# Attention keys' low parts doubled over both row halves in a two-layer transformer trunk

## The chip, the cores and the metric

The kernel runs on one core of one Trainium2 chip. The metric is the device time of one execution, in microseconds. PE is the engine of matrix products (PEld its weight loads), DVE and ACT do elementwise work, POOL a little of it, and SP issues most DMAs.

## The reference

Two layers (`DEPTH = 2`) on 512 tokens of width 1024. In each layer five attentions run on the same input, and a gated sum of them is projected, added to the input and normalised. Then a mixture of 16 experts (two for each token) follows, and a second norm.

```python
def hybrid_mixer(h, ...):
    h = x @ w_in                       # queries, keys, values of all branches
    o_sb   = stick_breaking_attention(q, k, v)          # 4 heads of 64
    o_moba = moba_attention(q, k, v, slopes)            # 4 heads of 64, causal here
    o_mla  = mla_attention(c_q, c_kv, k_rope, ...)      # 4 heads of 96
    o_nsa  = nsa_attention(q, kv, gates, ...)           # 4 heads of 64, two sets of shared keys
    o_mem  = memory_cross_attention(q_mem, mem, w)      # 4 heads of 64, 256 keys
    for i, o in enumerate((o_sb, o_moba, o_mla, o_nsa, o_mem)):
        merged += sigmoid(x @ w_gate[i] + b_gate[i]) * (o @ w_br[i])
    return merged @ w_out
```

A score is `q . k * scale`, with a slope times the distance in some branches; the weights of a query are the softmax of its scores (in stick breaking, a running product).

## The kernel before

Products are made from split numbers: every operand is kept as a high part (rounded to the type that PE takes at full rate) and a low part (what is left), and a product is the sum of high x high, high x low and low x high. `hi` (line 93) makes a high part, a copy on ACT; `lo` (line 108) makes a low part, a subtraction on DVE.

**Projections.** `fm_tile` (line 154) makes one [128 columns, 512 tokens] tile of `x @ w`: 24 matmuls at line 161, each 512 columns wide. Weights are loaded by SP, split on ACT and DVE, and used once. The gates (`gates`, line 770) are of this kind.

**Queries and keys.** A head has 64 numbers, half the height of PE. `q_stack` (line 204) puts a head's high query parts into its 64 rows and the low parts into the other 64. `k_pair` (line 212) gets two heads' keys from one psum tile and makes three tiles of the tag `qk`: for each head a tile with its high parts in both halves, and one tile `kl` in which each head's low parts lie in its own half. So one product over 128 rows gives q_hi k_hi + q_lo k_hi, and a second one over 64 rows gives q_hi k_lo. `std_passes` (line 318) lists the two passes. The compressed sparse attention makes its keys in `nsa_qkv` (lines 684 to 693) and already doubles the low parts there, but uses them through the same two passes.

**Scores.** `score_block` (line 232) takes 128 queries against L keys: the passes go into one psum bank of the tag `s` (two banks), through `mm` at line 116. DVE makes the minimum (line 246 with distances, 249 without), ACT the exponential (251), DVE the reciprocal and the scaled rows `ne` (252 to 256). `to_pt` (line 259) transposes them on PE (line 124) into a bank `pt`, and ACT and DVE split them into `pth` and `ptl`. At a head's end `causal_pv` (line 299) multiplies them with the values. L is 128, 256, 384 and 512 for a head's four blocks in the causal branches and 256 for each block of the memory's. The stick-breaking branch (line 403) has its own softmax substitute but the same two passes; the 96-wide latent attention (line 592) has three passes of 96 rows and doesn't use `k_pair`.

**Order.** `mixer` (line 904) weaves three generators by strings of letters in `orders` (line 1610): the attention of one branch (a), the gates of the branch before (g) and the projections of the next branch (q). Within this a scheduler orders the instructions and puts in the waits; every engine then works in the order of its own queue. Tiles of one tag share a number of slots given in `BUFS` (line 1592); a new tile waits until a slot is free. `qk` has 14 slots of 2 KB a partition, in the pool that is open during a layer's attentions. Around the experts other pools take its place.

Of the kernel before, what the change touches and what calls it, by code (L numbers as in the profile page):

```python
# [10 lines left out]
F32R = mybir.dt.float32r  # L11
# [7 lines left out]
P = 128  # L19
D = 1024  # L20
S = 512
# [4 lines left out]
ALPHA = (2.0 * DEPTH) ** 0.25  # L26
# [4 lines left out]
CAP = 112  # L31
# [39 lines left out]
class Trunk:  # L71
# [13 lines left out]
    # ---------------------------------------------------------------- tiles  # L85
# [6 lines left out]
    # ---------------------------------------------------------------- split  # L92
# [33 lines left out]
    # -------------------------------------------------------------- weights  # L126
    def load_w(self, src, shape, tag="rw", pool=None):
        """One raw piece of up to 4 KB a partition."""
        t = self.sb(pool or self.wp, [P, 1024 if tag == "rw" else 256], tag)
        n = 1  # L130
        for x in shape:
            n *= x
        v = t[:, :n]
        if len(shape) == 2:
            v = v.rearrange("p (a b) -> p a b", a=shape[0])
        if src is not None:
            self.loaded = self.nc.sync.dma_start(v, src)
        return v

    def split_w(self, raw, tag="wh", eng="dve", pool=None):  # L140
        """raw [P, a, b] -> its high and low parts, in one slot."""
# [11 lines left out]
    # feature-major tile of x @ w[:, cols]: w_hl is ([P, 8, M], [P, 8, M])  # L153
# [11 lines left out]
    def fm_chunk(self, w, c0, use, n=2, cut=1):  # L165
        """128 n columns of x @ w, feature-major: use(j, psum) for each tile."""
# [5 lines left out]
    def tm_chunk(self, w, c0, use, x=None, nt=NT, outer="k"):  # L172
        """256 columns of x @ w, token-major: use(t, psum [P, 256]). Two token tiles to a bank."""
        xh, xl = (self.xh, self.xl) if x is None else x
        o = [self.ps("f") for _ in range(nt // 2)]
        hl = {}

        def part(g, kk, t):
# [6 lines left out]
            for m, (a, b) in enumerate(((xh, h), (xh, l), (xl, h))):  # L185
                # one start a bank: it clears the whole bank's written bits
# [14 lines left out]
    # ------------------------------------------------------------ QKV parts  # L201
    H2 = (slice(0, 64), slice(64, 128))

    def q_stack(self, ps, rows, scale):
        """64 psum rows, scaled: their high parts stay in place, their low parts take the other half."""
# [6 lines left out]
    def k_pair(self, ps, n=S):  # L212
        """Two heads' keys: high parts doubled over both halves, a tile a head; low parts in place."""
        kh = [self.sb(self.ap, [P, S], "qk", F32R) for _ in range(2)]
        kl = self.sb(self.ap, [P, S], "qk", F32R)
        for r, k in zip(self.H2, kh):
            other = self.H2[r.start == 0]
            self.hi(k[r, :n], ps[r, :n])
            self.hi(k[other, :n], ps[r, :n])
            self.lo(kl[r, :n], ps[r, :n], k[r, :n])  # L220
        return [(kh[0], kl, self.H2[0]), (kh[1], kl, self.H2[1])]

    def v_split(self, ps, nh=4):
        """psum [P tok, nh*64] -> [P, nh, (hi 64 | lo 64)]."""
# [6 lines left out]
    # ------------------------------------------------------------ attention  # L231
    def score_block(self, i, L, passes, strip, slope=1.0, gate=None, causal=False):
        """Normalised probabilities [P q, L] in SBUF (fp32)."""
# [25 lines left out]
    def to_pt(self, e, nb, dst):  # L259
        """nb blocks of e [P q, nb*128], transposed and split: dst(hl) gives [P, nb, 128] views."""  # L260
# [8 lines left out]
    def pv_out(self, pv, o32, at):  # L269
        """[V_hi | V_lo] halves added into rows `at` of o32."""  # L270
# [19 lines left out]
    def causal_dst(self, pt, i, rev=False):  # L290
        # key tile j of query block i lies at columns (i + 3 j) * 128
# [7 lines left out]
    def causal_pv(self, pv, pt, vt, start, stop):  # L299
        """vt(j): [P, 128] stationary for key tile j."""  # L300
# [17 lines left out]
    def std_passes(self, q, k, qr=None):  # L318
        """Stacked queries on doubled keys, then the high queries (rows qr) on low keys (rows r)."""
        kh, kl, r = k  # L320
        return [(lambda sl: q[:, sl], lambda sl: kh[:, sl]), (lambda sl: q[r, sl], lambda sl: kl[r, sl])]

    # ------------------------------------------------------------- branches
# [26 lines left out]
    class _K:  # L350
        """[:, k, columns] of a list of tiles."""
# [51 lines left out]
    def sb_att(self, l, out):  # L403
        nc = self.nc
        for pr in range(2):
            o32 = self.o_tile()
            out.append(o32)
            for hh in range(2):
# [3 lines left out]
                for i in range(NT):  # L412
# [9 lines left out]
                    # u[j]: what all keys from j on leave; a key takes the difference  # L422
# [38 lines left out]
    # MLA  # L461
    def mla_qkv(self, l):
# [5 lines left out]
        # c_q (two tiles) and c_kv, feature-major, with their squares  # L468
        for j, c0 in ((2, 1792), (0, 1536), (1, 1664)):
# [6 lines left out]
            # sums of squares, token-major  # L476
# [11 lines left out]
        # k_rope | its halves swapped | the gates of the sparse attention  # L488
# [13 lines left out]
        # k rope: x cos + swapped x (-+ sin)  # L502
# [29 lines left out]
        # w_ukv -> [nope 4x64 | v 4x64]  # L532
# [32 lines left out]
        # w_uq per head [nope 64 | rope 32 | swapped 32]  # L565
# [42 lines left out]
    # NSA  # L608
    def nsa_qkv(self, l):
        nc, A = self.nc, self.A  # L610
        w = A["w_in"][l]
        # positional rows: [16, 128] = (pair, (parity, d)), doubled over partitions
# [16 lines left out]
        for m in range(2):  # L629
            x = self.sb(self.ap, [P, 16, 32], "ne")  # L630
            r = self.H2[m]
            for b in range(2):
                # windows n = 0..30 of 32 tokens, stride 16; token 2 a + b of each
# [8 lines left out]
        for m, nm in enumerate(("w_phi_k1", "w_phi_v1")):  # L642
# [6 lines left out]
            # gelu (tanh form): x/2 (1 + tanh(c (x + 0.044715 x^3)))  # L649
# [18 lines left out]
        # k_c duplicated over both halves: [kc_hi | kc_lo]  # L668
# [7 lines left out]
        # v_c of head h in rows 32 h  # L676
# [35 lines left out]
    def nsa_att(self, l, out):  # L712
        nc = self.nc
        # compressed scores, all heads and blocks: [P q, i, h, 32]
# [30 lines left out]
        for pr in range(2):  # L745
            o32 = self.o_tile()
            out.append(o32)
            for hh in range(2):
# [3 lines left out]
                for m in range(2):  # L752
                    pt = self.pt_tiles()
                    for i in range(NT):
                        e = self.score_block(i, P * (i + 1), self.std_passes(q, self.nk[m] + (self.H2[hh],)),
# [13 lines left out]
    # ------------------------------------------------------- gates and out  # L769
    def gates(self, l, b, o, first):  # L770
        """Adds sigmoid(x Wg + bg) * (o Wb) to merged (without the 0.5), 128 columns a step."""
# [24 lines left out]
    # ---------------------------------------------------------------- setup  # L796
# [21 lines left out]
    def setup_rest(self):  # L818
        """The constants that nothing needs at once."""
# [11 lines left out]
    def layer_cols(self, l):  # L831
        """Per-partition columns: 40 halved gate biases, g_cq (2), g_ckv, ln1 g and b (8 each)."""
# [15 lines left out]
    def x_tile(self, src, t, tag="f"):  # L848
        """Token tile t [P, 1024] into the transposed split x."""
# [10 lines left out]
    def weave(parts, order):  # L860
        """Runs the steps of generators in an order of their names, then the rest of each."""
# [6 lines left out]
    def start(self, l):  # L868
        """The layer's transposed input, the memory's keys and values, and what needs a token tile at a time."""
# [52 lines left out]
    def fill_rows(self, n, after):  # L922
        """Something finite in an expert's rows: its unused slots are read too."""
# [4 lines left out]
    # ------------------------------------------- output projection and norms  # L928
    def norm(self, st, eps=LN_EPS):
        """From the statistics of rows: minus their mean, the inverse of their deviation, minus the product."""  # L930
# [22 lines left out]
    def w_out(self, l, h_dram):  # L953
        """Output projection, residual, the first norm and the router: h1 token-major, its rows sent to experts.

        Two token tiles at a time share each split row block of the weights; the last blocks finish one tile, then the other."""
# [77 lines left out]
    def rows_done(self, t, o, hr, gb, pool):  # L1034
        """From the products of a tile: its rows' norm, logits and places. Yields how much later to go on."""
# [43 lines left out]
    # ------------------------------------------------------------------ moe  # L1079
    def router_w(self, l, pool):  # L1080
        """Router weights with the norm's gain folded in, their column sums, and the bias that its shift and theirs give."""
# [20 lines left out]
    def logits_in(self, x, half, pool):  # L1102
        """Half of the rows' columns, transposed."""
# [8 lines left out]
    def logits(self, o, xT, half):  # L1112
        """Adds the part of half of the rows' columns to the psum of the router's products."""
# [16 lines left out]
    def first_max(self, v, mx):  # L1130
        """Places of the largest (mx) of v [P, 4]: their priorities, and in column 4 the first one's."""
# [551 lines left out]
```

## Time and profile before

| | before |
|---|---|
| median of 3 runs, us | 1750.81 (1747.84 to 1752.13) |
| profiled execution, span, us | 1752.8 (no other time is given for it) |
| PE busy, us | 1644.5, 94% |
| PE weight loads busy, us | 1280.7, 73% |
| DVE busy, us | 1245.2, 71% |
| ACT busy, us | 896.2, 51% |
| matmuls | 7936 |

Busy time of PE is not the same as work: the profile's matmul durations overlap, and a matmul that waits for its own weight load counts as busy. How long PE takes for something is read from the starts of the instructions that follow each other. The attentions of the first layer lie between about 25 and 525 us, those of the second between 875 and 1400 us; the gates of the last branch, the output projection and the experts follow each.

### The profile page before, as it was taken

To read this page: it belongs to the slowest core of one execution; us is meant where nothing else is said; L and a number is where in the kernel's file an instruction comes from. 1 tells how busy PE (TensorE), PEld (TensorE's weight loads), DVE (VectorE), ACT (ScalarE), POOL (GpSimd) and SP (SyncE) were. 2 spreads that over 40 slices of the span, in tenths; PEclk is the share of its full clock that TensorE was granted. 3 is DMA by queue.
4 is the path that set the end of the run, shared out by engine and by line. 5 is a ranking of instruction groups with operands and counts; after the bars stand their busy time and mean duration, and the time that the engine had idled before them with its cause. 6 is when DMAs were issued, how large, how long until landed. Compare 5 with 4: busy or idle time off the path is not lost. (4 is left out here: it accounts for less than half of the span.)

```text
span 1752.8 us, 22824 instructions
## 1 busy us (share of the span) xinstructions
PE 1644.5 (94%) x7936; PEld 1280.7 (73%) x7936; DVE 1245.2 (71%) x2488; ACT 896.2 (51%) x1689; POOL 356.1 (20%) x261
## 2 busy tenths in 40 slices
PE   8999999999999987999699999999999998789994
PEld 7777877787778766666587787778877786676672
DVE  6666647765784689988687746587666757898876
ACT  5544446344463434888456334454444524358872
POOL 0000011111212254333410000110101113533345
PEclk9999999999999998999799999999999999899997
DMA  8232222353329547997642232223322286499943
GB/s 249 60 91 72 65 71 61 112 132 106 105 62 312 196 159 253 387 379 245 196 132 60 70 84 66 75 60 95 88 78 61 68 293 191 147 315 382 375 161 129
DMA packets 254561, 273.60 MB, mean 156 GB/s; under 512 B 38666, under 2 KB 191360, under 8 KB 254432
## 3 DMA queue, kind: packets, MB, share of 16 engines
q1 hardware_dynamic: 241032, 223.98, 40.2%
q0 software_dynamic: 13312, 47.98, 7.9%
q8 instruction: 67, 1.10, 0.3%
q14 instruction: 62, 0.51, 0.1%
q10 hardware_dynamic: 88, 0.03, 0.0%
HBM read 239.18 MB, written 32.77 MB: 155 GB/s over the span
## 5 line engine op out<-in xcount | busy, mean ns | idle before, releaser
L161 PE MATMUL f<-xh,wh 128*128 128x512 f32 (+2 forms) x1920 | 634.9, 400 | 1.6 <-ACT xh L97 0.9
L161 PEld LDWEIGHTS f<-xh,wh 128*128 128x128 f32 (+1 forms) x1920 | 354.4, 188 | 85.0 <-issue 5.2
L161 PE MATMUL f<-xl,wh 128*128 128x512 f32 (+2 forms) x960 | 383.6, 400 | 0.0
L791 POOL TENSOR_TENSOR mg<-mg,gt 128x512 f32<-128x512 f32 x64 | 96.3, 1505 | 1005.8 <-DVE gt L790 965.4
L112 DVE TENSOR_TENSOR wh<-rw,wh 128x1024 fp32r<-128x1024 f32 (+3 forms) x172 | 228.1, 1332 | 50.1 <-ACT wh L97 48.7
L161 PEld LDWEIGHTS f<-xl,wh 128*128 128x128 f32 (+1 forms) x960 | 180.6, 188 | 41.4 <-issue 3.5
L97 ACT CAST wh<-rw 128x1024 fp32r<-128x1024 f32 (+3 forms) x178 | 178.7, 1012 | 46.7 <-PE f L187 13.9
L781 ACT ACTIVATE gt<-f,bgh 128x512 f32<-128x512 f32 x80 | 55.1, 688 | 209.1 <-PE f L161 199.7
L116 PE MATMUL f<-wh,xh 128*112 128x512 f32 (+1 forms) x564 | 156.0, 404 | 5.0 <-DVE xh L112 2.7
L97 ACT CAST pth<-pt 128x128 fp32r<-128x128 f32 (+1 forms) x192 | 77.2, 418 | 110.4 <-PE pt L124 104.0
L116 PE MATMUL s<-qk,qk 128*128 128x256 f32 (+11 forms) x416 | 130.0, 367 | 0.7 <-DVE st L246 0.7
L116 PE MATMUL f<-oh,bh 128*128 128x512 f32 x480 | 130.3, 398 | 0.1
L116 PEld LDWEIGHTS f<-wh,xh 128*112 128x112 f32 (+1 forms) x564 | 98.7, 180 | 36.1 <-DVE wh L112 3.7
L116 PE MATMUL f<-eh,xh 128*112 128x512 f32 (+1 forms) x396 | 110.1, 404 | 10.6 <-DVE eh L112 10.6
L112 DVE TENSOR_TENSOR ptl<-pt,pth 128x128 fp32r<-128x128 f32 (+1 forms) x192 | 89.2, 475 | 42.2 <-ACT pth L97 39.8
L790 DVE SCALAR_TENSOR_TENSOR gt<-gt,f 128x512 f32<-128x512 f32 x64 | 43.8, 684 | 103.6 <-PE f L116 103.0
L116 PEld LDWEIGHTS s<-qk,qk 64*128 64x128 f32 (+2 forms) x416 | 75.7, 189 | 47.6 <-issue 28.5
L97 ACT CAST wh<-rp 128x1024 fp32r<-128x1024 f32 x84 | 87.4, 1053 | 38.3 <-PE pt L116 24.0
L112 DVE TENSOR_TENSOR wh<-rp,wh 128x1024 fp32r<-128x1024 f32 x70 | 94.9, 1365 | 13.2 <-ACT wh L97 12.6
L116 PEld LDWEIGHTS f<-oh,bh 128*128 128x128 f32 x480 | 88.0, 188 | 20.4 <-issue 1.2
L116 PEld LDWEIGHTS f<-eh,xh 128*112 128x112 f32 (+1 forms) x396 | 68.8, 179 | 31.4 <-DVE eh L112 12.3
L124 PE MATMUL pt<-ident,ne 128*128 128x128 f32 x472 | 82.9, 277 | 4.1 <-DVE ne L426 1.6
(366 smaller groups left out, 2832.4 us busy)
## 6 DMA issues: line engine op xcount, KB each, us to landing
rp<-in_w_up_dram SPq DMA_DIRECT2D x96, 512.0 KB, 14.2
rw<-in_w_gate_dram SPq DMA_DIRECT2D x80, 512.0 KB, 3.9
rp<-in_w_down_dram SPq DMA_DIRECT2D x48, 512.0 KB, 13.7
rw<-in_w_in_dram SPq DMA_DIRECT2D x38, 512.0 KB, 3.9
rw<-in_w_out_dram SPq DMA_DIRECT2D x32, 512.0 KB, 4.7
yd<-xl POOLq DMA_DIRECT2D x28, 448.0 KB, 7.0
xl<-xd POOLq DMA_DIRECT2D x24, 448.0 KB, 7.6
rb<-in_w_br_dram SPq DMA_DIRECT2D x80, 128.0 KB, 3.4
```

Source lines behind the costliest of these rows:

```text
L97: return nc.scalar.copy(out, in_)
L112: return e.tensor_tensor(out, in_, hi.bitcast(F32), ALU.subtract)
L116: self.nc.tensor.matmul(out, lhsT, rhs, start=start, stop=stop)
L124: self.nc.tensor.transpose(out, in_, self.ident[:k, :k])
L161: self.nc.tensor.matmul(o[:M, n], a[:, k, :M], b[:, k, n], start=c + k + m == 0, stop=k == KT - 1 and m == 2, skip_group_check=cut > 1)
L781: nc.scalar.activation(t, gp, AF.Tanh, bias=self.bgh[:, b * 8 + f : b * 8 + f + 1], scale=0.5)
L790: nc.vector.scalar_tensor_tensor(t, t, 1.0, bp, ALU.add, ALU.mult)
L791: i = nc.gpsimd.tensor_tensor(m, m, t, ALU.add)
```

## The change

`k_pair` gives each head its own low tile with the low parts in both halves. For the memory's 256 keys, high and low parts share one tile of 512 columns. `std_passes` multiplies the whole query tile with both, so that the second pass gives q_hi k_lo + q_lo k_lo over 128 rows. The compressed attention hands over its key tiles as they are. `qk` has 18 slots. The rest of the diff takes out comments.

```diff
     def k_pair(self, ps, n=S):
-        kh = [self.sb(self.ap, [P, S], "qk", F32R) for _ in range(2)]
-        kl = self.sb(self.ap, [P, S], "qk", F32R)
-        for r, k in zip(self.H2, kh):
+        out = []
+        for r in self.H2:
             other = self.H2[r.start == 0]
-            self.hi(k[r, :n], ps[r, :n])
-            self.hi(k[other, :n], ps[r, :n])
-            self.lo(kl[r, :n], ps[r, :n], k[r, :n])
-        return [(kh[0], kl, self.H2[0]), (kh[1], kl, self.H2[1])]
+            t = [self.sb(self.ap, [P, S], "qk", F32R) for _ in range(S // n - 1 or 2)]
+            kh, kl = t if len(t) == 2 else (t[0][:, :n], t[0][:, n:])
+            for o in (r, other):
+                self.hi(kh[o, :n], ps[r, :n])
+            for o in (r, other):
+                self.lo(kl[o, :n], ps[r, :n], kh[r, :n])
+            out.append((kh, kl))
+        return out
...
-    def std_passes(self, q, k, qr=None):
-        kh, kl, r = k
-        return [(lambda sl: q[:, sl], lambda sl: kh[:, sl]), (lambda sl: q[r, sl], lambda sl: kl[r, sl])]
+    def std_passes(self, q, k):
+        return [(lambda sl: q[:, sl], lambda sl, x=x: x[:, sl]) for x in k]
...
-                        e = self.score_block(i, P * (i + 1), self.std_passes(q, self.nk[m] + (self.H2[hh],)),
+                        e = self.score_block(i, P * (i + 1), self.std_passes(q, self.nk[m]),
...
-    BUFS = dict(rb=2, bh=2, gt=2, oo=4, oh=2, qk=14, v=6, ne=3, st=6, ot=2, mt=3, cp=2, uw=3,
+    BUFS = dict(rb=2, bh=2, gt=2, oo=4, oh=2, qk=18, v=6, ne=3, st=6, ot=2, mt=3, cp=2, uw=3,
```

## Rows read from the trace of the kernel before

**Rows 1.** The page's first line.
```profile
span 1752.8 us, 22824 instructions
```

**Rows 2.** Busy time by stretch: length, busy us (x count) by engine, clock, DMA.
```profile
25.00:525.00 500.00, 496.81 (x2428) 389.67 (x2426) 337.63 (x790) 244.87 (x553) 46.48 (x39) 0.99 0.32 89
...
875.00:1400.00 525.00, 519.78 (x2571) 409.14 (x2571) 358.33 (x827) 256.75 (x567) 44.19 (x31) 0.99 0.28 78
```

**Rows 3.** Waits of PE, 25 to 525 us, the longest: total us, times, longest.
```profile
PE pt L124 <- DVE ne L426: 0.8, 2, 0.5
```

**Rows 4.** Score passes' weight loads by shape: busy, mean ns, idle before, its end.
```profile
L116 PEld LDWEIGHTS s<-qk,qk 128*128 128x128 f32 x160 | 30.1, 188 | 10.9 <-DVE st L246 2.4 <-issue 1.2 <-ACT ne L251 0.5
L116 PEld LDWEIGHTS s<-qk,qk 64*128 64x128 f32 x160 | 29.2, 183 | 33.5 <-issue 27.3
...
L116 PEld LDWEIGHTS s<-qk,qk 96*128 96x128 f32 x96 | 16.3, 199 | 3.3 <-ACT ne L251 1.5
```

**Rows 5.** Timeline, weight loads around a 384-wide block: start us, length us, instruction.
```profile
268.10 0.19 PEld L116 LDWEIGHTS s<-qk,qk 128*128 128x128 f32 x1
268.54 0.18 PEld L116 LDWEIGHTS s<-qk,qk 64*128 64x128 f32 x1 [0.25 <-issue]
268.91 0.19 PEld L116 LDWEIGHTS f<-cp,uw 128*128 128x128 f32 x1 [0.19 <-issue]
269.02 0.19 PEld L161 LDWEIGHTS f<-xh,wh 128*128 128x128 f32 x1
```

**Rows 6.** Timeline, matmuls around blocks of 384, 256 (two) and 128.
```profile
268.27 0.71 PE L116 MATMUL s<-qk,qk 128*128 128x384 f32 x2
268.92 0.50 PE L116 MATMUL f<-cp,uw 128*128 128x512 f32 x1
269.25 0.39 PE L161 MATMUL f<-xh,wh 128*128 128x512 f32 x1
269.48 0.39 PE L161 MATMUL f<-xl,wh 128*128 128x512 f32 x1
...
924.68 1.21 PE L116 MATMUL s<-qk,qk 128*128 128x256 f32 x4
925.83 0.50 PE L161 MATMUL f<-xh,wh 128*128 128x512 f32 x1
926.17 0.39 PE L161 MATMUL f<-xl,wh 128*128 128x512 f32 x1
...
188.96 0.48 PE L116 MATMUL s<-qk,qk 128*128 128x128 f32 x2
189.37 0.50 PE L161 MATMUL f<-xh,wh 128*128 128x512 f32 x1
189.70 0.39 PE L161 MATMUL f<-xl,wh 128*128 128x512 f32 x1
```

**Rows 7.** Timeline, matmuls of full height, 384 and 256 columns wide.
```profile
371.94 0.35 PE L116 MATMUL pv<-ptl,v 128*128 128x384 f32 x1
372.12 0.28 PE L116 MATMUL pv<-pth,v 128*128 128x256 f32 x1
372.24 0.28 PE L116 MATMUL pv<-ptl,v 128*128 128x256 f32 x1
```

**Rows 8.** Waits of the weight loader, 25 to 525 us: total us, times, longest.
```profile
PEld pv L116 <- ACT pth L97: 2.5, 11, 0.4
PEld pt L124 <- DVE ne L254: 1.5, 4, 0.9
...
PEld pv L116 <- DVE ptl L112: 1.2, 5, 0.4
```

**Rows 9.** Low parts on DVE by shape: count, busy us, mean ns, idle before.
```profile
L112 DVE TENSOR_TENSOR qk<-f,qk 64x512 fp32r<-64x512 f32 x32 | 21.9, 685 | 13.5 <-ACT qk L97 13.0
...
L112 DVE TENSOR_TENSOR qk<-f,qk 64x256 fp32r<-64x256 f32 x8 | 3.4, 421 | 1.1 <-ACT qk L97 1.0
```

**Rows 10.** Busy time where layer two starts, columns as in rows 2.
```profile
850.00:875.00 25.00, 17.52 (x71) 13.76 (x71) 19.15 (x40) 12.95 (x29) 8.75 (x6) 0.69 0.46 141
```

## The prediction

> **What bounds the kernel now.** I read the page first: one core, a span of 1752.8 us [rows 1]. The busy times by stretch come second [rows 2], because the change touches only the attention of the two layers, and that runs from about 25 to 525 us and from 875 to 1400 us. The reader is to see that PE is busy there for 496.8 of 500 us and 519.8 of 525 us, while DVE works for two thirds of that time and ACT for half. Third, the waits of PE in the first of these stretches: the longest group is 0.8 us in 500 [rows 3]. So in attention the end is set by how long PE takes for its own queue, and the question is whether all of that time is work.
>
> It is not. In the weight loads by shape [rows 4] the three heights of the score passes stand apart. The 160 loads that are 64 rows high have 33.5 us of idle loader time before them, and 27.3 us of it ended for no reason that the profile shows ("issue"). The 160 loads of full height, from the same line and the same tiles, have 1.2 us of that kind, and the 96 loads that are 96 rows high show none. The timeline of one 384-wide block says how it comes about [rows 5]. The full-height load at 268.10 is done when its matmul starts at 268.27 [rows 6]. The 64-row load for the second pass does not run ahead like that: it begins at 268.54, together with its own matmul. The full-height load behind it begins only at 268.91, again with its matmul. The next one, at 269.02, is early again. So going to the half height and coming back each leave a weight load uncovered, and PE waits for it while it counts as busy.
>
> **The change, part by part.** The first pass of each block stays as it is. The second pass takes the whole stacked query tile against low keys that lie in both halves, so it loads the full height, and no pass of the kernel's scores is 64 rows high any more. The number of matmuls and loads stays the same. What a pair of height changes costs is read from starts, because the durations overlap [rows 6]. Undisturbed, 512 columns follow each other every 0.23 us (269.25 to 269.48), 384 columns every 0.18 us and 256 columns every 0.12 us [rows 7]; for 128 columns I take the 0.12 us of 256, which is a ceiling.
> 384 wide: from 268.27, the start of the full pass, to 269.25, when the second matmul after the block starts, 0.98 us pass; undisturbed it would be 0.18 + 0.18 + 0.23 = 0.59, so 0.39 us are lost.
> 256 wide: two blocks and one matmul take 924.68 to 926.17 = 1.49 us, where 4 x 0.12 + 0.23 = 0.71 would do: 0.78, or 0.39 us a block.
> 128 wide: 188.96 to 189.70 = 0.74 us against 0.12 + 0.12 + 0.23 = 0.47: 0.27 us.
> 512 wide: I take the 0.39 us of 384, since 256 and 384 agree.
> The code has 16 such blocks in each of the memory, the stick-breaking and the block-sparse attention and 32 in the compressed one, 80 a layer, 160 in all, as the loads are counted [rows 4]. The memory's are all 256 wide; in the others the four widths come equally often. That makes 64 blocks of 256 and 32 of each other width: 128 x 0.39 + 32 x 0.27 = 58.6 us of PE time that goes. This is the main term.
>
> What is late next is the softmax chain: score, minimum, exponential, reciprocal, scaling, then the transposes and the probability products on PE. PE works off other blocks and projections meanwhile. The loader shows where that cover is already used up: in the first layer it stood waiting 11 times for the high probabilities, 5 times for the low ones and 4 times for scaled rows [rows 8], though PE itself was still busy with the matmul before, so hardly any of it reached PE [rows 3]. When PE gets through the score passes sooner, such places become waits of PE. They are 20 a layer, 40 in all; I give back half of one block's saving, 0.2 us, at each: 8 us. The ends are nothing, if the waits merge, and 0.2 us at each of the 192 blocks (160 and the 32 of the 96-row attention, three loads each), 38 us.
>
> DVE gets one more subtraction per head in three attentions: 16 of 512 columns at 685 ns and 8 of 256 at 421 ns [rows 9], 14.3 us in all. The number of copies on ACT doesn't change. Behind each subtraction stand DVE's reductions of the running attention and the low parts of weights, and PE waits for those. The cover is DVE's idle third [rows 2]; without it the whole 14.3 us would count, and nothing is the other end. I take the share of blocks without slack, 40 of 192, of it: 3 us.
>
> The key and query slots go from 14 to 18. An attention with four heads needs 12 tiles where it needed 10, the memory's 8 instead of 10, so there is never less room than before, and PE hardly waits in these stretches [rows 3]: nothing. The pool grows by four tiles, though, and what is opened over it before and after the experts moves with it. The nearest row is the stretch in which layer two starts, where PE is busy for 17.5 of 25 us [rows 10]: the 7.5 us could go or come once more. I take nothing and keep both ends. No DMA is added or moved, and no step goes past another queue.
>
> The sum is -58.6 + 8 + 3 = -47.6 us. The span that these rows come from lies 2.0 us above the median of the three runs, 1750.8 us, and the page shows nothing around it; taken from the median, 1703 us.
>
> Two rules speak against the change. The rows give the main term without them. The Trainium skill, TensorE: Matmul & The Clock Gate, section Why this matters for your kernels, has it that a matmul with few rows takes as long as one with all 128; by it the main term would be nothing. The rows differ from that here, for a half-height pass between full ones. The same page, section Part 3 on packing small matmuls, says that a weight load runs beside a matmul in flight only if it is for other row groups; by it two full-height passes in a row would hide no load. The full-height load at 269.02 runs beside the full-height matmul of 268.92 [rows 5, 6], so the rows differ from that as well.
>
> **The rivals.**
> (a) The forecast: PE stays the bound and keeps most of what it gains, 1703 us, between 1690 and 1717.
> (b) The chain takes half or more back: waits of 0.1 to 0.2 us on average at the 192 blocks, 19 to 38 us, and the low parts with 3; 1714 to 1733, about 1724. For it speaks that in the first layer 20 loads already arrive ahead of their data [rows 8]; against it that DVE and ACT have a third and a half of their time free [rows 2].
> (c) Slower: the chain paces attention altogether. From an average wait of 58.6 / 192 = 0.31 us a block on, all of the gain is gone, and if DVE is then the pace, its 14.3 us add in full: 1765 us. Against it: PE's longest group of waits is 0.8 us in 500 now [rows 3].
> (d) The height is not the cause: the lost time hangs on something that stays, such as two passes of one bank in a row. Then PE gains nothing and the low parts cost some: about 1755. Against it: the 96-row passes are such passes, three to a bank, and lose nothing to "issue" [rows 4].
> (e) The second load stays uncovered once, as it reads the same queries as the first. One of two exposed loads remains, half the term: 58.6 / 2 - 11 = 18 us, 1732. Against it stand the full-height loads with one stationary tile used twice, as at 269.02. By the row-group rule above it would go this way.
>
> **How the numbers follow.** Chances: (a) 0.62, (b) 0.26, (c) 0.05, (d) 0.04, (e) 0.03. A run of this kernel scatters by some 0.2%, and 0.3%, 5 us, is about what can be told from no change. Faster are (a), (b) and (e), 0.91; within 0.3% is (d), 0.04; slower is (c), 0.05. The predicted time is that of (a). The range goes from the whole main term with nothing given back, 1692, less some 3 us for the scatter and for a start of layer two that gains, to (b)'s 38 us given back, 1750.8 - 58.6 + 38 = 1730, and it leaves out (c), (d) and the edges: 1689 to 1731.
>
> **What would show it.** Right: the score loads are all 128 rows high and have hardly any "issue" idle time; a 384-wide block with the matmul behind it takes about 0.59 instead of 0.98 us; both attention stretches are shorter by some 24 us each, and the expert stretches as long as before. Step two is right if the waits of PE for DVE and ACT in these stretches grow from a few to some 5 us a layer, and wrong if they stay as small as now (the gain then nears 59 us) or grow past 15. It would be wrong altogether if the spacing of the score passes stayed where it is, or if PE's busy share in attention fell below 95%.

## The result, and the profile after

The median after is 1727.9 us (1724.7 to 1732.4, four runs) against 1751.5 us of the kernel before beside it: a ratio of 0.9867, with an interval of 0.9844 to 0.9889, or 23.6 us less. The sign was forecast rightly and the size was not: 47.6 us were forecast, and the time came out where rival (b) had it.

Everything that the change was to do to the score passes happened. The page of the kernel after, its span and its busy times:

```profile
span 1723.8 us, 22844 instructions
...
PE 1608.3 (93%) x7936; PEld 1272.9 (74%) x7936; DVE 1257.8 (73%) x2512; ACT 893.2 (52%) x1689; POOL 356.6 (21%) x261
```

The score passes' weight loads by shape, with the columns of [rows 4]. All 320 are of full height now, and no idle time before them ends in "issue" any more; what is left ended with the reductions on DVE and the exponentials on ACT:

```profile
L116 PEld LDWEIGHTS s<-qk,qk 128*128 128x128 f32 x320 | 51.3, 189 | 21.8 <-DVE st L249 9.3 <-ACT ne L254 4.4 <-ACT ne L422 2.0
...
L116 PEld LDWEIGHTS s<-qk,qk 96*128 96x128 f32 x96 | 15.6, 200 | 4.8 <-ACT ne L254 3.2
```

The timeline of a 384-wide block and what follows it, matmuls first and then the weight loads, to be held against [rows 5, 6]:

```profile
124.17 0.40 PE L116 MATMUL pv<-pth,v 128*128 128x512 f32 x1
124.41 0.52 PE L116 MATMUL s<-qk,qk 128*128 128x384 f32 x2
124.76 0.62 PE L161 MATMUL f<-xh,wh 128*128 128x512 f32 x2
125.22 0.40 PE L161 MATMUL f<-xl,wh 128*128 128x512 f32 x1
```
```profile
124.25 0.35 PEld L116 LDWEIGHTS s<-qk,qk 128*128 128x128 f32 x2
124.58 0.37 PEld L161 LDWEIGHTS f<-xh,wh 128*128 128x128 f32 x2
125.00 0.19 PEld L161 LDWEIGHTS f<-xl,wh 128*128 128x128 f32 x1
```

From 124.41 to 125.22 the block and two matmuls of 512 columns take 0.81 us, where 2 x 0.18 + 2 x 0.23 = 0.82 is undisturbed. The two loads of the block are issued in one go from 124.25, ahead of their matmuls, and the loads behind them are early too.

The time, however, shrank less than this. The two stretches of attention, columns as in [rows 2]:

```profile
25.00:515.00 490.00, 478.70 (x2430) 385.87 (x2428) 345.38 (x803) 243.65 (x555) 46.67 (x39) 0.99 0.33 91
863.00:1373.00 510.00, 497.52 (x2579) 401.98 (x2578) 366.19 (x842) 256.15 (x567) 44.37 (x31) 1.00 0.28 81
```

They are the stretches of [rows 2], cut to nearly the same matmuls (2430 and 2579 against 2428 and 2571). Their lengths sum to 1000 us where it was 1025. PE's busy time in them fell from 1016.6 to 976.2 us, by 40.4, and its idle time rose from 8.4 to 23.8 us, by 15.4. So the profile itself says that something gives back, and its list of PE's waits from 25 to 515 us says what, in the form of [rows 3]:

```profile
PE pt L124 <- DVE ne L428: 1.9, 6, 0.5
PE s L116 <- ACT ne L254: 1.5, 1, 1.5
PE s L116 <- DVE st L249: 1.3, 3, 0.8
PE pt L124 <- DVE ne L257: 1.2, 2, 0.8
PE f L187 <- DVE qk L112: 1.2, 1, 1.2
PE f L620 <- ACT gt L783: 1.1, 1, 1.1
```

Two kinds lead: transposes (`pt`) that wait until DVE has scaled their rows, and score passes (`s`) that wait until a psum bank has been read by an earlier block. Both are steps of the softmax chain. One is of another sort, `f L187 <- DVE qk`: a projection behind a low part. The times at which the same head ends in both traces place the gain: the last head of layer one ends 10.0 us earlier (529.2 to 519.2) and that of layer two 27.0 us earlier (1396.4 to 1369.4), so the two stretches are shorter by 10 and 17 us, where some 24 each were to show that the forecast was right. Between the last attention product of layer one and the first score pass of layer two lie 388.7 us in both traces, so the experts gave and took nothing.

### The profile page after: what moved, and what is told of

Read it like the earlier page. It is cut to its first block, busy times and chain, and to the rows that moved or that the text cites. A ratio compares the mean times of both kernels' runs of the same rounds, so it can differ in the third digit from the quotient of the medians.

```text
span 1723.8 us, 22844 instructions
## 1 busy us (share of the span) xinstructions
PE 1608.3 (93%) x7936; PEld 1272.9 (74%) x7936; DVE 1257.8 (73%) x2512; ACT 893.2 (52%) x1689; POOL 356.6 (21%) x261
## 5 line engine op out<-in xcount | busy, mean ns | idle before, releaser
L112 DVE TENSOR_TENSOR wh<-rw,wh 128x1024 fp32r<-128x1024 f32 (+3 forms) x172 | 228.1, 1332 | 52.1 <-ACT wh L97 50.8
L116 PE MATMUL s<-qk,qk 128*128 128x256 f32 (+7 forms) x416 | 98.3, 334 | 5.7 <-DVE st L249 2.6
L112 DVE TENSOR_TENSOR wh<-rp,wh 128x1024 fp32r<-128x1024 f32 x70 | 95.0, 1366 | 10.9 <-ACT wh L97 10.0
L116 PEld LDWEIGHTS s<-qk,qk 128*128 128x128 f32 (+1 forms) x416 | 66.9, 192 | 26.5 <-DVE st L249 9.3
```

Of the source, the lines that this page charges most:

```text
L112: return e.tensor_tensor(out, in_, hi.bitcast(F32), ALU.subtract)
L116: self.nc.tensor.matmul(out, lhsT, rhs, start=start, stop=stop)
```

## The experiments

All times are medians. The kernel before stood between 1751.3 and 1752.9 us beside them, and the ratio is to it, with its 95% interval. "Worth of the height" is the difference between two kernels that differ only in whether the second pass has 64 rows or 128.

### The parts one at a time

`e1_passes` is the kernel before with the second pass at full height and nothing else: no low part more, 14 slots. As the low tile is still shared by two heads, its second pass adds q_lo times the low keys of the neighbouring head.

```diff
-        return [(lambda sl: q[:, sl], lambda sl: kh[:, sl]), (lambda sl: q[r, sl], lambda sl: kl[r, sl])]
+        return [(lambda sl: q[:, sl], lambda sl: kh[:, sl]), (lambda sl: q[:, sl], lambda sl: kl[:, sl])]
```

> The kernel before, but the second score pass multiplies the whole query tile with the shared low tile over 128 rows: the product of the low queries with the other head's low keys comes on top (in the compressed attention, whose low keys are already doubled, that of its own). No further subtraction, 14 slots, and the order of every queue nearly that of before. Chain theory (the softmax chain takes back what PE gains): the gain of the whole change comes here too, about 24 us, 1724 to 1731 us. Companion theory (the height gives its 59 us or nearly, and the additional low parts and the new order of the queues take it back): 45 us or more, 1695 to 1707 us. Height not the cause: 1750 us.

1716.6 us, 0.9806 (0.9786 to 0.9826). The height alone is worth 35.5 us, neither 58.6 nor the 50 that my give-back would have left.

`e2_lows` is the counterpart: the change's tiles and slots, with the second pass at 64 rows.

```diff
+        kh, kl = k
-        return [(lambda sl: q[:, sl], lambda sl, x=x: x[:, sl]) for x in k]
+        return [(lambda sl: q[:, sl], lambda sl: kh[:, sl]), (lambda sl: q[r, sl], lambda sl: kl[r, sl])]
```

> The changed kernel, but with the second pass 64 rows high as before (high queries on the own half of the doubled low keys): the additional low parts, the 18 slots and the changed kernel's queue order alone. Chain theory: the companions cost little, 1748 to 1756 us, as before. Companion theory: 20 to 35 us slower than before, 1770 to 1785 us.

1762.8 us, 1.0073 (1.0053 to 1.0094). What comes along with the height costs 10.7 us, and the height in this company is worth 1762.8 - 1727.9 = 34.9 us, nearly the 35.5 of `e1_passes`. The height and its companions add.

`e3_slots` is the kernel before with `qk=18` for `qk=14`, and `e4_after14` the kernel after with `qk=14` for `qk=18`.

> The kernel before with 18 instead of 14 key and query slots, nothing else. Chain theory: 1748 to 1755 us. Companion theory, if it is the slots that change order or layout: up to 20 us slower; if it is the low parts: 1748 to 1755 us.

> The changed kernel with 14 slots again, so that tiles of the next attention wait for those of the running one. Chain theory: 1724 to 1735 us, the slots matter little. Companion theory with the slots as its cause: 1700 to 1715 us; with the low parts as its cause: 1724 to 1735 us.

`e3_slots`: 1758.9 us, 1.0052 (1.0033 to 1.0071), so four slots that nothing needs cost 6.8 us. `e4_after14`: 1722.0 us, 0.9846 (0.9822 to 0.9871), 5.9 us below the kernel after. If the slots are the 5.9 us, the low parts are the step from `e1_passes` to `e4_after14`, 5.4 us. The three terms, -35.5 + 5.4 + 5.9 = -24.2 us, come to the measured -23.6 by the way they were formed, so the sum confirms none of them. A second reading of the low parts is the step from `e3_slots` to `e2_lows`: 3.9 us. The six runs of `e4_after14` lie between 1716.9 and 1728.4 us and overlap those of the kernel after, so the 5.9 us are not clear of the noise; the next section says what separates them.

### The slots: place or order

`e17_pad` opens an unused tile of 8 KB a partition in the pool of the key tiles, which is what four slots more take up, and leaves the slots at 14.

```diff
-        self.bq, self.bk, self.bv = [], [], []
+        self.bq, self.bk, self.bv = [], [], []; pad = self.ap.tile([P, 2048], F32, tag="pad", name=f"pad{l}"); self.nc.gpsimd.memset(pad[:, 0:1], 0.0)
```

> The kernel before with 14 key and query slots and one unused tile of 8 KB a partition in the same pool (one column of it set on POOL), as much as four more slots take: the place of what shares the memory, without the freedom of more slots. If the 18 slots cost their 7 us by the place, 1756 to 1762 us; if by the order of the queues, 1749 to 1755 us.

1750.0 us, 0.9991 (0.9977 to 1.0004): nothing. The order of PE's 7936 matmuls is that of the kernel before. So where the pools lie costs nothing, and what costs in `e3_slots` is that with room for more tiles the scheduler lays the queues out differently. For the kernel after the traces say something else. Its heads' ends stand against those of `e4_after14` as follows: up to the first head of the latent attention in layer one the kernel after is 2 to 3 us ahead (344.7 against 347.9), by the last one 6.3 us behind (433.8 against 427.5), and the 6.3 stay to the end of that layer's attention. The windows of that stretch, the kernel after first and then `e4_after14`, which stands at a slightly earlier time:

```profile
331.00:370.00 39.00, 36.97 (x209) 30.98 (x209) 27.63 (x84) 19.11 (x56) 3.63 (x4) 0.91 0.50 125
```
```profile
329.00:366.00 37.00, 36.07 (x223) 30.78 (x222) 30.98 (x90) 21.91 (x61) 3.77 (x4) 1.00 0.53 132
```

With 18 slots PE does 209 matmuls in 39 us, with 14 it does 223 in 37; it idles 2.0 us instead of 0.9, and the granted clock is 0.91 instead of 1.00. The lower clock belongs to one part, 363.0 to 373.3 us, in which half of the clock was granted, 1.2 GHz and not 2.4; PE had been busy for 17.9 of the 18 us before it:

```profile
363.00:373.00 10.00, 9.63 (x33) 7.92 (x33) 4.94 (x20) 3.24 (x15) 0.67 (x1) 0.50 0.66 155
```

Matmuls of 512 columns follow each other every 0.43 us there, not every 0.23. With two shorter parts, from 315.2 and from 1172.0 us, this trace has 17 us of attention at half the clock. Less the undisturbed spacing, 8.0 us are lost in them. The trace of `e4_after14` has no such part in its attentions, and the two spans are 9.0 us apart (1723.8 and 1714.8).

The other runs agree: three of `e4_after14` took 1716.9 to 1718.7 us at a mean granted clock of 0.973 to 0.974, and three took 1725.3 to 1728.4 at 0.967 to 0.968. All four of the kernel after are at 0.964 to 0.968, and the two at 0.967 and 0.968 took 1725.9 and 1724.7 us. At an equal clock, then, no difference between the two is seen. Whether the order with 18 slots makes the clock fall more often isn't shown.

In `e3_slots`, at 0.970 to 0.973 beside 0.969 to 0.974 of the kernel before, the clock is no explanation, and its 6.8 us stand as the price of the slots.

The timeline of the kernel after shows the longest of PE's waits here, ahead of the long part:

```profile
338.20 0.48 PE L161 MATMUL f<-xh,wh 128*128 128x512 f32 x1
338.30 1.05 ACT L97 CAST wh<-rw 128x1024 fp32r<-128x1024 f32 x1 [1.57 <-DMA rw<-in_w_gate_dram]
339.25 0.47 ACT L97 CAST pth<-pt 128x384 fp32r<-128x384 f32 x1
...
339.62 0.37 ACT L254 ACTIVATE ne<-s,st 128x128 f32<-128x128 f32 x1
...
340.14 0.79 PE L116 MATMUL s<-qk,qk 96*128 96x384 f32 x3 [1.46 <-ACT ne L254]
```

A score pass waits 1.46 us for a bank; the exponential that frees it stands on ACT behind a weight's high part, which stood 1.57 us waiting for its DMA. A wait of this kind occurs with 14 slots too (0.9 us), so it is an example of what an unlucky order costs and a small part of the 6 us.

### Where the worth of the height goes

In the traces 7925 of the 7936 matmuls of `e1_passes` can be matched in order with those of the kernel before. For each the time to the start of the next one was taken, less the undisturbed 0.234, 0.175, 0.117 or 0.109 us for 512, 384, 256 or 128 columns. At the matmuls next to a former change of height (144 of the 158 ahead of a 64-row pass are first passes), the surplus:

```
                         kernel before   e1_passes
matmul before the pass (158) 19.3 us        3.7
second pass (158)            29.0           2.5
matmul after the block (130) 13.2           3.3
sum                          61.5           9.4
```

So 52.1 us went where the forecast said. Elsewhere the times ahead of transposes grew by 10.1 us and those ahead of score passes by 5.7 us, and all else together is small: 36 us are left, beside 35.5 between the medians and 39.6 between the two spans. Of the 9.4 us that stayed, 3.3 stand at 47 matmuls whose own weight load had waited for DVE or ACT. The pair `e2_lows` and the kernel after is cleaner still: PE, DVE and ACT start their instructions in the same order in both, all 7936 matmuls among them. There the surplus falls from 62.8 to 10.2 us, the times ahead of transposes grow by 8.9 us and those ahead of score passes by 6.3. With the order equal, the order can't be what gives back. The groups of PE by line show the same growth as idle time. Busy us and mean ns of one | idle before and what ended it; the kernel before, `e1_passes`, the kernel after:

```profile
L116 PE MATMUL s<-qk,qk 128*128 128x256 f32 (+11 forms) x416 | 130.0, 367 | 0.7 <-DVE st L246 0.7
...
L124 PE MATMUL pt<-ident,ne 128*128 128x128 f32 x472 | 82.9, 277 | 4.1 <-DVE ne L426 1.6 <-DVE ne L254 1.6 <-DVE ne L256 0.5
```
```profile
L116 PE MATMUL s<-qk,qk 128*128 128x256 f32 (+7 forms) x416 | 99.0, 332 | 3.9 <-DVE st L246 2.6 <-ACT ne L420 0.7
...
L124 PE MATMUL pt<-ident,ne 128*128 128x128 f32 x472 | 84.1, 280 | 9.2 <-DVE ne L426 3.8 <-DVE ne L254 3.4 <-DVE st L252 0.6
```
```profile
L116 PE MATMUL s<-qk,qk 128*128 128x256 f32 (+7 forms) x416 | 98.3, 334 | 5.7 <-DVE st L249 2.6 <-ACT ne L254 1.5 <-ACT ne L422 0.8
...
L124 PE MATMUL pt<-ident,ne 128*128 128x128 f32 x472 | 83.7, 279 | 8.5 <-DVE ne L428 3.8 <-DVE ne L257 2.5 <-DVE st L255 0.7
```

Score passes are busy for 31 us less and wait 3 to 5 us more; transposes are as busy as before and wait 4 to 5 us more. Idle time is only what PE stands after its last matmul has ended; of the 10.1 us ahead of transposes it shows 5.1, and the other half lies under matmuls that count as busy while the load behind them waits.

If these waits hold what is missing, then whatever relieves the chain must raise the worth of the height. Five reliefs were tried, each on `e1_passes` and on the kernel before.

**Less work on DVE: no scaling of rows.** `e7_nonorm` and `e8_nonorm_b` (the kernel before) leave out the reciprocal and the scaling of the probabilities, so their weights aren't normalised.

```diff
-        nc.vector.reciprocal(st[:, 2:3], st[:, 1:2])
-        if gate is None:
-            nc.vector.tensor_scalar(e[:, :L], e[:, :L], st[:, 2:3], None, ALU.mult)
-        else:
-            nc.vector.tensor_scalar(e[:, :L], e[:, :L], st[:, 2:3], gate, ALU.mult, ALU.mult)
```

> Full-height second passes as in the run of the passes alone, and the softmax chain made shorter: it leaves out the reciprocal and the scaling of each block's rows by it and the gate, so the rows go to the transposes unscaled (160 blocks, two DVE instructions each). To be compared with the same kernel with 64-row passes, whose queues have nearly the same order. Chain theory: with a shorter chain less of PE's gain is given back; the full height is worth 45 to 57 us between the two, where it is worth 35.5 with the scaling in. If the give-back has another cause (the score passes, the order of PE's queue, DMAs), it stays at 33 to 38 us.

> The kernel before, with the reciprocal and the scaling left out, 64-row passes. Chain theory: PE is the bound here, so a shorter chain gives little, 1740 to 1752 us. If the chain bounds already with 64-row passes: 1735 us or less.

1725.4 us, 0.9845 (0.9827 to 0.9864), and 1765.3 us, 1.0075 (1.0049 to 1.0101): the height is worth 39.9 us, not the 45 to 57 of the chain theory. It is no clear rise over 35.5 either: the runs of `e8_nonorm_b` go from 1754.6 us at a clock of 0.972 to 1769.1 at 0.965, and the two profiled executions, both at 0.971, are 32.0 us apart (1756.0 and 1724.0). Both kernels are slower with less to do, by 8.8 and 12.5 us. The order of the queues is planned anew with every edit, and the new order may cost more than the work that left it; what does wasn't found.

**Less work on DVE: the gates' low parts on POOL.** `e5_pool` and `e6_pool_b` (the kernel before).

```diff
-            h, lw = self.split_w(self.load_w(self.cols(A["w_gate"][l, b], f * P, P), (KT, P)))
+            h, lw = self.split_w(self.load_w(self.cols(A["w_gate"][l, b], f * P, P), (KT, P)), eng="pool")
```

> Full-height second passes as in the run of the passes alone, with the low parts of the gates' weights (80 subtractions of 128x1024, 1.3 us each) on POOL and not on DVE. To be compared with the same kernel with 64-row passes. If what lengthens the chain is DVE's queue, the full height is worth 40 to 52 us between the two; if the chain is a matter of its own steps, it stays near 35 us.

> The kernel before with the low parts of the gates' weights on POOL, 64-row passes. Both theories: within 8 us of before, 1744 to 1760 us, since PE is the bound; slower if the split weights now come too late.

1765.4 us, 1.0079 (1.0062 to 1.0095), and 1794.3 us, 1.0249 (1.0225 to 1.0274): both far slower, and the height is worth only 28.9 us. The low parts of weights in `e6_pool_b` by engine:

```profile
L112 POOL TENSOR_TENSOR wh<-rw,wh 128x1024 fp32r<-128x1024 f32 x86 | 209.1, 2431 | 681.8 <-ACT wh L97 608.7 <-PE s L124 22.7 <-ACT pth L97 19.7
L112 DVE TENSOR_TENSOR wh<-rw,wh 128x1024 fp32r<-128x1024 f32 x84 | 113.3, 1354 | 20.9 <-ACT wh L97 20.2
```

One takes 2431 ns on POOL and 1354 ns on DVE; 80 of the 86 were moved, 6 were on POOL before. No wait of PE or of its loader for a low part on POOL is in this trace. In the first layer's attention PE waits longest ahead of transposes (3.3 and 3.2 us for `ne`). That the weights of the gates, PE's filler between the blocks, are now placed later is a guess. This pair doesn't say what the chain on DVE costs.

**More slots for the rows.** `e9_ne5` and `e14_ne5_b` (the kernel before) have `ne=5` for `ne=3`.

> Passes alone at full height, with 5 slots for the scaled rows and nothing else. If the slots of the scaled rows hold score passes back, 1700 to 1712 us; otherwise as without them, 1713 to 1720 us.

> The kernel before, 64-row passes, with 5 slots for the scaled rows. Both theories: 1745 to 1758 us.

1713.3 us, 0.9776 (0.9757 to 0.9795), and 1753.4 us, 1.0004 (0.9992 to 1.0015): a worth of 40.2 us. `e9_ne5` itself is only 3.3 us below `e1_passes`, and their runs overlap.

**Transposes one block later.** `e12_late` and `e13_late_b` (the kernel before) also have `ne=5`, and transpose a block's rows only when the next block's scores have been issued. In all four kinds of heads:

```diff
-            self.to_pt(e, i + 1, self.causal_dst(pt, i))
+            if i:
+                self.to_pt(old, i, self.causal_dst(pt, i - 1))
+            old = e
...
+        self.to_pt(old, NT, self.causal_dst(pt, NT - 1))
```

> Passes alone at full height, with the transposes of a block written behind the score passes of the next block (not right behind its own) and 5 slots for the scaled rows, so that PE has more other work between a block's scores and its transposes. Slack theory (the order of PE's queue leaves about 4 us between a block's scores and its transposes, the half-height switches were part of these 4 us, and without them the rows come too late): with more work between, the full height is worth 45 to 57 us against the same kernel with 64-row passes, and this run is at 1700 to 1710 us. Rival (the give-back is not in the transposes' place in the queue): 33 to 38 us between the two.

> The kernel before, 64-row passes, with the transposes written one block later and 5 slots for the scaled rows. Slack theory: 1745 to 1758 us, since PE waits for little there as it is. Rival: the same.

1716.8 us, 0.9796 (0.978 to 0.9813), and 1757.1 us, 1.0029 (1.0018 to 1.004): a worth of 40.4 us. The transposes of the two, `e13_late_b` first:

```profile
L124 PE MATMUL pt<-ident,ne 128*128 128x128 f32 x472 | 83.5, 279 | 4.2 <-DVE ne L433 2.4 <-DVE ne L254 1.0 <-DVE ne L431 0.5
```
```profile
L124 PE MATMUL pt<-ident,ne 128*128 128x128 f32 x472 | 83.6, 279 | 5.1 <-DVE ne L433 3.1 <-DVE ne L254 1.0 <-DVE ne L431 0.5
```

The height makes them wait 0.9 us more now, where it was 5.1 us; by starts the give-back ahead of transposes fell from 10.1 to 3.9 us. Part of this is the slots: in `e9_ne5` against `e14_ne5_b` it is 7.0 us by starts and 2.0 us of waiting. That the scaled rows were late is shown by the rest. The time gained, 4.9 us of worth, is no more than the slots alone gave.

**A third bank for scores.** `e15_bank` and `e16_bank_b` (the kernel before) have `ne=5` and put the second block's scores of each head into the bank of the probability products.

```diff
-        s = self.ps("s")
+        s = self.ps("pv" if i == 1 else "s")
```

> Passes alone at full height with 5 slots for the scaled rows, and the second block of each head scores into the bank that otherwise only the value products use, so that score blocks have three banks and not two. Bank theory (score passes wait for a bank that the softmax of two blocks before still reads, and that is what is left of the give-back): the full height is worth 44 to 55 us against the same kernel with 64-row passes, where it is worth 40 with two banks, and this run is at 1698 to 1708 us. Rival (banks don't matter): 36 to 42 us.

> The kernel before, 64-row passes, 5 slots for the scaled rows and the third score bank. Bank theory: 1745 to 1757 us, PE being the bound. Rival: the same.

1720.8 us, 0.9825 (0.9803 to 0.9848), and 1766.0 us, 1.0087 (1.0064 to 1.0111): a worth of 45.2 us, the highest, and within what the bank theory named; the time is not (1698 to 1708). The rows of `e15_bank`:

```profile
L124 PE MATMUL pt<-ident,ne 128*128 128x128 f32 x472 | 85.5, 284 | 10.9 <-DVE ne L254 6.4 <-DVE ne L426 3.8
L116 PE MATMUL s<-qk,qk 128*128 128x512 f32 (+6 forms) x328 | 82.2, 343 | 1.3 <-ACT ne L420 0.8
```

The waits of the score passes went down, to 1.3 us for 328 passes in the `s` banks and 0.8 for the 88 in the other, from 5.5 for all 416 in `e9_ne5`, and the transposes, next in line, wait 10.9 instead of 8.2. The two kernels are slower than their partners without it, by 7.6 us at full height and by 12.6 at 64 rows, so the higher worth comes from the 64-row kernel losing more. By starts the times ahead of the products grew by some 5 us in both; the rest of the loss isn't placed.

**Both.** `e18_both` and `e19_both_b` (the kernel before) join the late transposes and the third bank.

> Passes alone at full height, with all three: 5 slots for the scaled rows, the third score bank, and the transposes written one block later. If the waits for rows and banks together are the give-back, the full height is worth 47 to 58 us against the same kernel with 64-row passes (40 with the late transposes, 45 with the third bank). Rival (something else holds the rest): 40 to 46 us.

> The same three with 64-row passes. Both theories: 1755 to 1772 us, the order costing some us as with each alone.

1721.5 us, 0.9825 (0.9805 to 0.9845), and 1763.3 us, 1.0073 (1.0054 to 1.0092): a worth of 41.9 us where the two reliefs together should have given 47 or more. They don't add.

**A better version.** `e9_ne5` beats both kernels at 1713.3 us, with the neighbour's low keys in its second pass, as in `e1_passes`. `e20_after14ne5` is the kernel after, with its own tiles, at `qk=14` and `ne=5`.

> The changed kernel with its doubled low parts, 14 key and query slots and 5 slots for the scaled rows: what the change would be with the better of the slot counts. 1714 to 1721 us if the effects add (1722 with 14 slots, less the 3 that 5 slots gave the passes alone).

1716.7 us, 0.9798 (0.9779 to 0.9817): 11.2 us below the kernel after without a change to its products. Its runs, at a clock of 0.971 to 0.975, took 1713.4 to 1719.6 us, which is not clearly less than the faster three of `e4_after14`.

## Why the prediction was right and wrong

**The bound and the main term were right.** The half-height passes did leave loads uncovered, and their height is the cause. The 58.6 us worked out from five timelines stand against a surplus of 61.5 us at those places in the whole trace, and 52.1 of it went. Rival (d) is out by `e1_passes` and `e2_lows`: height alone brings 35 us with either set of tiles. Rival (e) named 1732 us, close to the time that came, but the two loads of the block at 124.25 run ahead of their matmuls, and no half of the loss stayed. The time alone would have confused it with (b); the spacing doesn't. The Trainium skill, TensorE: Matmul & The Clock Gate, section Part 3, lets a weight load overlap, in its list of what overlaps, only with a matmul on other row groups, by which it would have gone the way of (e); the full-height loads at 124.25 and 124.58 run beside full-height matmuls, so this trace differs from it.

**The give-back of 8 us was mis-sized, and this is the step that failed.** I took 0.2 us at the 40 places where a weight load already stood before its data [rows 8]. Measured on the height alone, 61.5 - 35.5 = 26 us of the surplus did not reach the end, 0.135 us on average at each of the 192 blocks. By starts 15.8 us of it, twice the 8, came back as longer times ahead of transposes and score passes, and 9.4 stayed at the old places. The count of 40 left out one of the two kinds of waits: score passes, for which the loader stood waiting too.

```profile
PEld s L116 <- DVE st L246: 1.2, 3, 0.7
...
PEld s L116 <- ACT ne L251: 1.0, 4, 0.4
```

These 7 places of layer one stand in the same list as [rows 8], and the times ahead of score passes grew by 5.7 us. So rival (b) had the mechanism, from the bound of 38 us that the prediction had worked out and then set aside; its price of 0.1 to 0.2 us a block holds for the 26 us and is too high for the 15.8 (0.08). That the time also fell next to its 1724 us is partly luck: the kernel after ran at a lower clock or paid for its slots, and (b) counted on neither. The argument against (b), that DVE and ACT are idle for a third and a half of the time [rows 2], was the wrong measure: PE waited for DVE and ACT more often although both stayed idle that much, so an engine with idle time can still be late for the next block. The sign that I set was nearly kept: PE's idle time grew by 7.7 us a layer, where "some 5" were to confirm 8 us and more than 15 to refute it. It saw only part of the loss, since a load that waits behind a running matmul leaves PE busy.

**The low parts were near their size.** They have 48 subtractions at 686 ns and 16 at 422 ns now, against 32 and 8 [rows 9]: 14.4 us more on DVE, as worked out. Of them 3.9 to 5.4 us reached the end by the two readings, where I took 3; with the faster three runs of `e4_after14` it would be 1 to 2. The difference from 3 is within the noise.

```profile
L112 DVE TENSOR_TENSOR qk<-f,qk 64x512 fp32r<-64x512 f32 x48 | 33.0, 686 | 11.0 <-ACT qk L97 10.2
...
L112 DVE TENSOR_TENSOR qk<-f,qk 64x256 fp32r<-64x256 f32 x16 | 6.7, 422 | 0.4
```

**The slots were not free.** "Never less room than before" is true and was no argument: room beyond the need changed the order in which the scheduler put things, for 6.8 us in the kernel before. In the changed kernel the 5.9 us can't be told from the lower clock. The bound of 7.5 us held it, but for another reason, the pools' places, which `e17_pad` rules out.

So of the 24 us that were forecast and didn't come, 15 belong to the height: 50.6 us net were forecast for it and 35.5 came, because 52.1 and not 58.6 went and 15.8 and not 8 came back. The other 8 to 9 are the low parts, the slots and the lower clock, and how they divide isn't shown. With (b) at 0.26 and (a) at 0.62 I had the two in the wrong order.

**What stays open.** The chain's waits are shown as the holder of part of the give-back: with PE, DVE and ACT working in the same order they grow by 15 us; those ahead of transposes shrink with the late transposes, and those ahead of score passes with the third bank. The worth rises from 35.5 to between 40 and 45 us with these reliefs. A worth is the difference of two medians, each good to some 3.5 us, so that steps of 5 us are at the edge of what can be told, and only the 45.2 of the third bank is well clear of 35.5. No relief brought it to 61. From one pair to the next the queues are laid out anew and the clock differs, so whether the rest would go with the chain isn't settled, nor why the kernels without scaling are slower.

## What to carry to other kernels

Where an engine is nearly always busy in a stretch, a cut of its time is paid out only as far as the chain behind it can follow, so price the give-back at every block that passes through the chain and not only at those that wait already. In a kernel whose order is planned by a scheduler, a buffer count is part of the schedule: measure a larger one by itself, and leave it where it was unless something waits for it. Before a few microseconds between two kernels are put down to their code, hold the granted clocks of their runs side by side. Judge the mechanism by the spacing of starts, since two rivals can agree in the total time.

## What was not expected of the hardware

The same subtraction of 128x1024 numbers took 2431 ns on POOL and 1354 ns on DVE in one kernel, and with 80 of them moved to POOL the kernel lost 41 to 49 us, although POOL was idle enough (busy for 121 of 500 us in the first layer's attention). Runs of one and the same kernel, `e4_after14`, fell into two groups some 9 us apart, the slower at a mean granted clock of 0.967 to 0.968 and the faster at 0.973 to 0.974. For the rest, what the rows showed of the heights held: 64-row passes between full ones lost 61.5 us at 158 of 160 blocks, full-height ones next to nothing by themselves.
